# Other orders in a layer's opening and its linear attention, and value products issued one step later in the windowed attention

## The chip, the cores and the metric

The kernel runs on one core of one Trainium2 chip. The core has a matrix engine (TensorE, PE in the profile; its weight loads are PEld), a vector engine (VectorE, DVE), a scalar engine (ScalarE, ACT), a slower general engine (GpSimd, POOL) and a sequencer that issues transfers (SyncE, SP). They run side by side, each takes its own instructions in order, and they wait for each other with semaphores. Products are summed in PSUM, 8 banks of 128 x 512 numbers; everything else lies in SBUF. The metric is the device time of one execution in microseconds; the median of three runs counts.

## The reference, cut to what matters

One layer of a diffusion backbone: 256 latent tokens and 256 context tokens, width 2048, batch 1, one layer. Weights and activations are 32-bit.

```python
mod_x = split(silu(c) @ w_mod + b_mod, 6); mod_c = split(silu(c_ctx) @ w_mod + b_mod, 6)
h  = rms_norm(x, g_mix) * (1 + mod_x[1]) + mod_x[0]        # latent; the context likewise
qa, ka, va, qb, kb, vb, rb, lrf, lrb, gate_a, gate_b = split(h @ w_in)
gf = log_sigmoid(lrf @ w_gate_f + b_gate_f) / 16            # decay of the linear attention
gb = log_sigmoid(lrb @ w_gate_b + b_gate_b) / 16            # and of its backward direction
# A: windowed attention, 16 heads of 128 in 4 groups; a query block sees latent and context keys
o_attn = softmax([scores(qa, ka) in the window, scores(qa, cka), sink]) @ [va, cva]
# B: gated linear attention, 4 heads, keys 256 wide, values 512 wide, both directions
o_gla = latent_gla(qb, kb, vb, gf, gb, states left by the context)
y = sigmoid(gate_a) * (o_attn @ w_attn_o) + sigmoid(gate_b) * ((rms_norm(o_gla) * silu(rb)) @ w_gla_o)
x = x + mod_x[2] * (y @ w_out)
x = x + mod_x[5] * conv_ffn(rms_norm(x, g_ffn) * (1 + mod_x[4]) + mod_x[3])
```

## The kernel before

**Products.** Every large product is done in halves: an operand a is split into a rounded part and a remainder (`split`, line 60: a copy on ACT, a subtraction on DVE), and three products are summed, high by high, low by high, high by low. Weights come from memory as tiles of 256 x 512 numbers (`raw`, seven buffers, tag "raw"), and `wsplit_raw` (line 207) makes `whi` on ACT and `wlo` on DVE, three buffers each. `proj_T` (line 263) and `proj_nat` (line 222) go through a projection tile by tile. At the start of each weight tile they call `tick()`, and between its high and its low half `midway()` or a function given as `mid`. Eight tiles make a block of 512 columns, so a block has 16 such places, 0 to 15, even ones at a tile's start and odd ones in its middle. In blocks with 512-wide products a tile is 16 products ahead of its middle and 8 behind it.

**Side work.** `aside()` (line 156) advances a generator that stands in `beside`, by a rate: at each place the rate is added, and for each whole one the generator goes to its next `yield`. Matrix products of side work carry a lower bound, the last projection product issued (`pin`, `after`); apart from that a scheduler orders each engine's instructions when the program is built, by priority (program order) and by when it estimates their operands to be ready. In the opening (until `opening.clear()`, line 675) PE's order is the order of the program. `bank(..., side=True)` gives one of three PSUM banks for side work. SBUF tiles of side work come from tags with few buffers: "fa" four, "fb" four, "fc" six; large tiles from `big`, 16 buffers.

**The opening** (lines 531 to 675). Latent tokens `xr` are loaded, transposed; `square_sums` makes squares and adds them up with products by ones (`pr`), `factor_row` makes the norm's factors (`rrow`) of it. Shift and scale come column group by column group: `mod_both` (line 313) loads `mraw`, multiplies (`pm`), transposes on DVE (`mtr`), and its last step `end` folds with one more product (`pcol`) and copies into `scale1`, `shift1`. `groups` are 2, 2, 4, 4 and 4 of the 16 column tiles of the model's width. For group 0, `mods[0]` holds (a0, a1, ea) for the scale and (b0, b1, eb) for the shift. `idle(n)` issues n transposes of an identity that nobody reads (`warm`). `affine_scale` and `affine_shift` turn `xr` into h with its halves (`h00hi`, `h00lo`, ...), and the projections QB, KB and VB (queries, keys and values of the linear attention, first half) follow group by group; line 616's loop does groups 1 to 4. Within group 1 the eight steps of group 2's shift and scale are spread over six places (`steps`, `also`, `mid`, lines 631 to 649). All loads of the opening are issued by SP in the order of the program (`chain`).

**Linear attention** (lines 740 to 928). Four heads, one beside each of four projection blocks: head 0 beside the second half of the keys (`kb_block`), heads 1 to 3 beside the values (`v_block`). `gla_A` makes, as side work: four gates (two directions, two halves of the key width; product `pz`, four passes on ACT into `ge` and `gm`, an addition on DVE into `segs` and one on POOL into `gc`), then eight levels. Level lv builds decayed queries and keys (`q2`, `k2`) for segments of 2^lv tokens: exponentials on ACT, products and running sums (`segs`) on DVE; the products of the level before (`pa`) go to PE at the same time and are merged on DVE. Scans over the context (`kf`, `kg`) stand beside the levels. Behind the last level come the products with the context states, and `gla_o` multiplies with the values (`po`). With rate 0.97 the generator is first advanced at place 1: gates at places 1 to 4, levels 0 to 7 at 5 to 12, the last level's products at 13, nothing at 14, the context's products at 15.

**Windowed attention** (`attend`, line 1007). Beside a projection block, for two query blocks t: scores (`pS`) of four heads, softmax on DVE and ACT, and then for four key blocks k: four transposes (`ptp`), their split into `pth` and `ptl` (tag "fb"), three value products into `poa`. A `yield` stands behind k = 1 and k = 3.

The rest (projections of the outputs, merging, output projection, and the feed-forward part with its convolution) is not touched.

Of the kernel before, what the change touches and what calls it, by code (L numbers as in the profile page):

```python
# [31 lines left out]
def layer_kernel(ctx, tc, A, out):  # L32
# [280 lines left out]
    def mod_both(part, t0, n, dst, put=None):  # L313
# [5 lines left out]
        def step(k0):  # L319
            if k0 == 0:  # L320
                a.append(bank(f"pm{part}_{t0}", (P, w), side=True))
            raw = M("mraw", [P, nk, w])
            src = A["w_mod01"][part, t0 + k0 // nk].rearrange("p (c d) -> p c d", c=nk)
            if t0 < 4 and part == 0 and k0:
                load(raw[:, 0:nk // 2, :], src[:, 0:nk // 2, :])
                load(raw[:, nk // 2:nk, :], src[:, nk // 2:nk, :])
            else:
                load(raw, src)
            for k in range(nk):
                kt = k0 + k  # L330
# [97 lines left out]
    kbt = M("kb0", [P, 4, 512])  # L428
    vb0 = M("vb0", [P, 4, 512])

    def square_sums(s):

        pr = bank("pr", (P, T), side=True)
        parts, whole = [], None
        for i in range(4):
            x_ = xr[2 * s + i // 2][:, (i % 2) * 4:(i % 2) * 4 + 4, :]
            q = wr.tile([P, 4, T], F32, name="sq", tag="raw")
            if s + i:
                j = S.activation(q, x_, AF.Square).ins
                if s and i in (0, 2):  # L440
                    in_order(evicted[i + 1], j)
            else:
                V.tensor_tensor(q, x_, x_, op=ALU.mult)
                parts.extend(q[:, k, :] for k in range(4))
                continue
            h = q[:, 0:2, :]
# [91 lines left out]
    opening[:] = [pe_seq(PE.transpose(warm[:, 0:P], ident, ident)).ins]  # L538
# [12 lines left out]
    b0()  # L551
    affine_scale(0, *groups[0])
    idle(6)
    b1()
    raws = [first_w(i) for i in range(2)]
    idle(4)
# [59 lines left out]
    for gi, (t0, n) in enumerate(groups):  # L616
# [8 lines left out]
        if gi + 1 < len(groups):  # L625
# [2 lines left out]
            bg_rate[:] = [1.4 * len(bg_steps) / ticks + 0.01, 0.0]  # L628
            if gi == 1:
                bg_rate[:] = [0.0, 0.0]  # L630
                steps = iter([1, 2, 1, 4, 0, 0])

                def next_columns():
                    if pend:
                        pend.pop(0)()

                def scale_2():
                    next_columns()
                    for s in range(2):
                        affine_scale(s, *groups[2])  # L640

                also = iter([next_columns] * 3 + [scale_2, next_columns, lambda: affine_shift(0, *groups[2])])

                def mid():
                    pin[0] = last[0]
                    next(also)()
                    for _ in range(next(steps)):
                        bg_steps.pop(0)()
                    pin[0] = None
# [87 lines left out]
                         b.rearrange("p (f t) -> p f t", f=2), AF.Copy, scale=1.0 / 16)  # L737
        return eq

    def gla_A(h, kb, qb, res):  # L740
        k_ = kb[:, (h % 2) * 2:(h % 2) * 2 + 2, 0:T]
        kc = kb[:, (h % 2) * 2:(h % 2) * 2 + 2, T:2 * T]
        q_ = qb[:, 2 * h:2 * h + 2, :]
        R = M("segs", [P, 4, 2, T])
        PF, SB, SX, PX = (R[:, i] for i in range(4))
        G.memset(R[:, 2:4], 0.0)
        gc = []
        for d in range(2):
            g_ = W2("fc", "gc", [P, 2, T])
            for dt in range(2):  # L750
                f = 2 * h + dt
                pz = bank("pz", side=True)
# [5 lines left out]
                S.activation(mn, pz, AF.Relu, scale=-1.0, bias=b)  # L758
                S.activation(e, e, AF.Exp, scale=-1.0)
                S.activation(e, e, AF.Ln, bias=ones[:, 0:1])  # L760
                V.tensor_tensor((PF if d == 0 else SB)[:, dt, :], mn[:, 0:T], e[:, 0:T], op=ALU.add)
                G.tensor_tensor(g_[:, dt, :], mn[:, T:2 * T], e[:, T:2 * T], op=ALU.add)
                yield
            gc.append(g_)

        kf = W2("fb", "kf", [P, 2, T])
        kg = W2("fb", "kg", [P, 2, T])

# [87 lines left out]
            S.activation(dst, e, AF.Exp, scale=-1.0 / 16)  # L856
# [150 lines left out]
    def attend(g, qT):  # L1007
# [3 lines left out]
        for t in range(2):  # L1011
# [354 lines left out]
```

## Time and profile before

| | us |
|---|---|
| median of three runs | 1974.27 (1974.04 to 1974.33) |
| profiled execution, its own time | 1973.72 |
| its span, first to last instruction | 1972.0 |
| PE busy | 1952.8 |
| DVE busy | 1396.9 |
| ACT busy | 971.6 |
| stretch 0 to 207 us (opening) | PE busy 196.3 |
| stretch 207 to 462 us (linear attention) | PE busy 251.6 of 255 |
| stretch 584 to 787 us (most of the windowed attention) | PE busy 202.7 of 203 |

A row of the profile tells the place in the program (L95 is line 95; `mm_b`, which issues all products of side work, is L95, and `mm`, the projections, L83; transposes of side work are L98), the engine, the operation, what it writes and reads, and its form. In a timeline the first two numbers are the start from the span's beginning and the time until the last of the merged instructions ended, x is their count, and square brackets hold idle time of the engine before it and what ended that. In a list of waits the numbers are the total, the count and the longest. The end of a matmul is modelled, and matmuls overlap; their starts are measured. "fp32" products and transposes take other steps than the rounded "fp32r" ones of the projections.

### The profile page before, as it was taken

To read this page: it belongs to the slowest core of one execution; us is meant where nothing else is said; L and a number is where in the kernel's file an instruction comes from. 1 tells how busy PE (TensorE), PEld (TensorE's weight loads), DVE (VectorE), ACT (ScalarE), POOL (GpSimd) and SP (SyncE) were. 2 spreads that over 40 slices of the span, in tenths; PEclk is the share of its full clock that TensorE was granted. 3 is DMA by queue.
4 is the path that set the end of the run, shared out by engine and by line. 5 is a ranking of instruction groups with operands and counts; after the bars stand their busy time and mean duration, and the time that the engine had idled before them with its cause. 6 is when DMAs were issued, how large, how long until landed. Compare 5 with 4: busy or idle time off the path is not lost.

```text
span 1972.0 us, 27091 instructions
## 1 busy us (share of the span) xinstructions
PE 1952.8 (99%) x10304; PEld 1635.6 (83%) x10304; DVE 1396.9 (71%) x2150; ACT 971.6 (49%) x1415; POOL 39.9 (2%) x60
## 2 busy tenths in 40 slices
PE   8999999999999999999999999999999999999999
PEld 6679988888887777888888888888888888888887
DVE  5756855785768998777776467989886545677754
ACT  5223655462346565444444445755555334555533
POOL 0010000020000000000000000000000000000000
PEclk9999999999999999999999999999999999999999
DMA  9975222226654466899997677688786556666563
GB/s 392 412 255 176 69 66 71 79 84 210 212 162 126 129 208 220 297 299 307 312 310 237 238 246 252 193 276 284 263 275 224 192 193 191 186 188 191 188 212 114
DMA packets 182867, 420.90 MB, mean 213 GB/s; under 512 B 12512, under 2 KB 12736, under 8 KB 177744
## 3 DMA queue, kind: packets, MB, share of 16 engines
q1 hardware_dynamic: 181200, 413.45, 63.7%
q0 software_dynamic: 1360, 5.54, 1.0%
q8 instruction: 81, 1.33, 0.3%
q14 instruction: 50, 0.41, 0.1%
q10 hardware_dynamic: 176, 0.17, 0.0%
HBM read 416.98 MB, written 2.13 MB: 213 GB/s over the span
## 4 chain that ended last, share of the span: by engine, by line
PE 94%; DVE 3%; ACT 1%; DMA 1%; issue 1%; ACTq 0%; DVEq 0%
PE acc L83 72%; PE accs L83 12%; PE pa L95 2%; PE poa L95 1%; PE pS L95 1%; PE po L95 1%; PE pm L95 1%; DVE wlo L212 1%; PE ptp L98 1%; DMA mraw<-in_w_mod 1%; ACT whi L211 0%; DVE q L831 0%; PE pto L98 0%; DMA pack<-in_k_pack 0%; DVE k L838 0%
## 5 line engine op out<-in xcount | busy, mean ns | idle before, releaser
L212 DVE TENSOR_TENSOR wlo<-raw,whi 128x1024 fp32r<-128x1024 f32 x568 | 694.0, 1223 | 426.5 <-ACT whi L211 387.8
L211 ACT ACTIVATE whi<-raw 128x1024 fp32r<-128x1024 f32 x568 | 601.1, 1059 | 785.1 <-PE acc L83 605.0
L83 PE MATMUL accs<-h,whi 128*128 128x512 f32 x704 | 176.3, 392 | 0.0
L83 PE MATMUL acc<-h,whi 128*128 128x512 f32 x640 | 160.4, 392 | 0.0
L83 PEld LDWEIGHTS accs<-h,whi 128*128 128x128 f32 x704 | 126.6, 189 | 22.6
L83 PE MATMUL acc<-whi,h01hi 128*128 128x512 f32 x352 | 139.7, 397 | 0.0
L83 PE MATMUL acc<-whi,h00hi 128*128 128x512 f32 x352 | 139.2, 395 | 0.0
L83 PE MATMUL acc<-whi,h01lo 128*128 128x512 f32 x352 | 138.4, 393 | 0.0
L83 PE MATMUL acc<-whi,h00lo 128*128 128x512 f32 x352 | 137.6, 391 | 0.0
L83 PE MATMUL acc<-whi,al 128*128 128x512 f32 x352 | 137.0, 389 | 0.0
L83 PE MATMUL acc<-whi,ah 128*128 128x512 f32 x352 | 137.0, 389 | 0.0
L83 PEld LDWEIGHTS acc<-h,whi 128*128 128x128 f32 x640 | 115.1, 189 | 20.6
L83 PEld LDWEIGHTS accs<-h,wlo 128*128 128x128 f32 x704 | 96.0, 190 | 6.9
L83 PE MATMUL acc<-wlo,h01hi 128*128 128x512 f32 x352 | 99.0, 396 | 0.0
L83 PE MATMUL accs<-h,wlo 128*128 128x256 f32 x704 | 98.2, 282 | 0.0
L83 PE MATMUL acc<-wlo,h00hi 128*128 128x512 f32 x352 | 98.1, 394 | 0.0
L83 PE MATMUL acc<-wlo,ah 128*128 128x512 f32 x352 | 94.3, 389 | 0.0
L83 PEld LDWEIGHTS acc<-h,wlo 128*128 128x128 f32 x640 | 87.4, 190 | 6.3
L83 PE MATMUL acc<-h,wlo 128*128 128x256 f32 x640 | 89.4, 282 | 0.0
L376 DVE CUSTOM_DVE_ANT_0 raw<-raw,csrow,pack 128x1024 f32<-128x1024 f32 x64 | 81.2, 1278 | 0.0
L83 PEld LDWEIGHTS acc<-whi,al 128*128 128x128 f32 x352 | 66.1, 188 | 13.7
L83 PEld LDWEIGHTS acc<-whi,ah 128*128 128x128 f32 x352 | 66.1, 188 | 13.7
(376 smaller groups left out, 3553.0 us busy)
## 6 DMA issues: line engine op xcount, KB each, us to landing
raw<-in_w_in SPq DMA_DIRECT2D x204, 512.0 KB, 4.5
raw<-in_w_up SPq DMA_DIRECT2D x176, 512.0 KB, 4.2
raw<-in_w_modT SPq DMA_DIRECT2D x128, 512.0 KB, 4.6
raw<-in_w_down SPq DMA_DIRECT2D x88, 512.0 KB, 3.6
mraw<-in_w_mod SPq DMA_DIRECT2D x30, 1024.0 KB, 12.5
raw<-in_w_attn_o SPq DMA_DIRECT2D x32, 512.0 KB, 5.3
raw<-in_w_gla_o SPq DMA_DIRECT2D x32, 512.0 KB, 5.4
raw<-in_w_out SPq DMA_DIRECT2D x32, 512.0 KB, 4.4
```

The source lines that it names most:

```text
L83: r = pe_seq(PE.matmul(*a, **k))
L95: return pe_seq(after(PE.matmul(*a, **k)))
L98: return pe_seq(after(PE.transpose(*a)))
L211: j = S.activation(hi[:, 0:n, :], raw[:, 0:n, :], AF.Copy).ins
L212: i = V.tensor_tensor(lo[:, 0:n, :], raw[:, 0:n, :], hi[:, 0:n, :].bitcast(F32), op=ALU.subtract).ins
L376: i0 = V.tensor_tensor_reduce(out=raws[i], in0=raws[i], in1=row[0], scale=1.0, scalar=d if h else bmod[:, b0:b0 + 1], op0=ALU.mult, op1=AL ...
```

## The change

In the opening: the second half of the shift weights of groups 0 and 1 is loaded in one transfer instead of two; the product passes a0 and a1 stand between the sums of squares instead of behind them; 14 of the fillers are left out (6, 4 and 4 of 6); `gm1` is ordered behind the first square. In group 1, the fourth of the four steps at one place goes to the next place, and the folding of the shift with it to the one after.

In the linear attention: the gates become a generator of their own, `gla_gates`. Head 0 has its gates at places 0 to 3, its levels at 4, 6, 7, 8, 9, 10, 11, 12, and two gates of head 1 at 13 and 14. Heads 1 to 3 have their other two gates at 0 and 1, levels at 2, 4, 5, 7, 8, 10, 11, 12, the last level's products at 13, the context's products at 15, and the first two gates of the next head at 9 and 14. The rate is 1.

In the windowed attention: the three value products of key block k are issued behind the transposes and the split of block k + 1.

```diff
-            src = A["w_mod01"][part, t0 + k0 // nk].rearrange("p (c d) -> p c d", c=nk)
-            if t0 < 4 and part == 0 and k0:
-                load(raw[:, 0:nk // 2, :], src[:, 0:nk // 2, :])
-                load(raw[:, nk // 2:nk, :], src[:, nk // 2:nk, :])
-            else:
-                load(raw, src)
+            load(raw, A["w_mod01"][part, t0 + k0 // nk].rearrange("p (c d) -> p c d", c=nk))
...
-    add_up(0, 6)
-    V.tensor_scalar(gm1, gmix, -0.5, None, op0=ALU.mult)
+    add_up(0, 4)
+    in_order(squared[0], V.tensor_scalar(gm1, gmix, -0.5, None, op0=ALU.mult).ins)
     (a0, a1, ea), (b0, b1, eb) = mods[0]
+    a0()
+    add_up(4, 6)
+    a1()
     add_up(6, 9)
     factor_row(pr)
-    a0()
-    idle(6)
-    a1()
-    idle(4)
     ea()
     b0()
     affine_scale(0, *groups[0])
-    idle(6)
+    idle(2)
     b1()
...
-                steps = iter([1, 2, 1, 4, 0, 0])
+                steps = iter([1, 2, 1, 3, 1, 0])
...
-                also = iter([next_columns] * 3 + [scale_2, next_columns, lambda: affine_shift(0, *groups[2])])
+                def shift_2():
+                    next_columns()
+                    affine_shift(0, *groups[2])
+
+                also = iter([next_columns] * 3 + [scale_2, next_columns, shift_2])
...
-    def gla_A(h, kb, qb, res):
+    def gla_gates(h):
         R = M("segs", [P, 4, 2, T])
         G.memset(R[:, 2:4], 0.0)
         gc = []
+        yield R, gc
         for d in range(2):
-            g_ = W2("fc", "gc", [P, 2, T])
+            gc.append(W2("fc", "gc", [P, 2, T]))
             for dt in range(2):
...
-        yield
         yield
         pa = bank("pa", (P, 2, T), side=True)
...
+    def gate(h):
+        if h == 4:
+            return
+        if h not in gates:
+            it = gla_gates(h)
+            gates[h] = next(it), it
+        next(gates[h][1])
+
     def with_gla(h, kb, block):
-        res = []
-        beside[:] = [gla_A(h, kb, qbt, res), 0.97, 0.0]
+        res, own = [], []
+
+        def level():
+            if not own:
+                own.append(gla_A(h, kb, qbt, *gates[h][0], res))
+            next(own[0], None)
+
+        this, following = lambda: gate(h), lambda: gate(h + 1)
+        places = {i: [this] for i in ((0, 1, 2, 3) if h == 0 else (0, 1))}
+        for i in (4, 6, 7, 8, 9, 10, 11, 12) if h == 0 else (2, 4, 5, 7, 8, 10, 11, 12):
+            places[i] = [level]
+        places.update({13: [level], 14: [following], 15: [level]})
+        places.setdefault(13 if h == 0 else 9, []).append(following)
+
+        def along():
+            for i in range(16):
+                for fn in places.get(i, ()):
+                    fn()
+                yield
+
+        beside[:] = [along(), 1.0, 0.0]
...
+            def values(k, th, tl):
+                vk_h, vk_l = vah[:, k, g * P:(g + 1) * P], val[:, k, g * P:(g + 1) * P]
+                mm_b(po, vk_h, th, start=(k == 0), stop=False)
+                mm_b(po, vk_h, tl, start=False, stop=False)
+                mm_b(po, vk_l, th, start=False, stop=(k == 3))
+
+            ready = None
             for k in range(4):
...
                 split(th, tl, pf)
-                vk_h, vk_l = vah[:, k, g * P:(g + 1) * P], val[:, k, g * P:(g + 1) * P]
-                mm_b(po, vk_h, th, start=(k == 0), stop=False)
-                mm_b(po, vk_h, tl, start=False, stop=False)
-                mm_b(po, vk_l, th, start=False, stop=(k == 3))
+                if ready is not None:
+                    values(*ready)
+                ready = k, th, tl
                 if k in (1, 3):
                     yield
+            values(*ready)
```

More of the change, by code (lines that the diff above doesn't have):

```diff
@@ L429, in layer_kernel @@
     vb0 = M("vb0", [P, 4, 512])
+    squared = []
     def square_sums(s):
@@ L442, in square_sums @@
             else:
-                V.tensor_tensor(q, x_, x_, op=ALU.mult)
+                squared.append(V.tensor_tensor(q, x_, x_, op=ALU.mult).ins)
                 parts.extend(q[:, k, :] for k in range(4))
@@ L738, in q_evac @@
         return eq
-    def gla_A(h, kb, qb, res):
-        k_ = kb[:, (h % 2) * 2:(h % 2) * 2 + 2, 0:T]
-        kc = kb[:, (h % 2) * 2:(h % 2) * 2 + 2, T:2 * T]
-        q_ = qb[:, 2 * h:2 * h + 2, :]
+    def gla_gates(h):
         R = M("segs", [P, 4, 2, T])
-        PF, SB, SX, PX = (R[:, i] for i in range(4))
         G.memset(R[:, 2:4], 0.0)
         gc = []
+        yield R, gc
         for d in range(2):
-            g_ = W2("fc", "gc", [P, 2, T])
+            gc.append(W2("fc", "gc", [P, 2, T]))
             for dt in range(2):
@@ L760, in gla_A @@
                 S.activation(e, e, AF.Ln, bias=ones[:, 0:1])
-                V.tensor_tensor((PF if d == 0 else SB)[:, dt, :], mn[:, 0:T], e[:, 0:T], op=ALU.add)
-                G.tensor_tensor(g_[:, dt, :], mn[:, T:2 * T], e[:, T:2 * T], op=ALU.add)
+                V.tensor_tensor(R[:, d, dt, :], mn[:, 0:T], e[:, 0:T], op=ALU.add)
+                G.tensor_tensor(gc[d][:, dt, :], mn[:, T:2 * T], e[:, T:2 * T], op=ALU.add)
                 yield
-            gc.append(g_)
+    def gla_A(h, kb, qb, R, gc, res):
+        k_ = kb[:, (h % 2) * 2:(h % 2) * 2 + 2, 0:T]
+        kc = kb[:, (h % 2) * 2:(h % 2) * 2 + 2, T:2 * T]
+        q_ = qb[:, 2 * h:2 * h + 2, :]
+        PF, SB, SX, PX = (R[:, i] for i in range(4))
         kf = W2("fb", "kf", [P, 2, T])
@@ L903, in layer_kernel @@
         q_evac(i // 2)(i % 2, qb0[i])
-    def with_gla(h, kb, block):
-        res = []
-        beside[:] = [gla_A(h, kb, qbt, res), 0.97, 0.0]
+    gates = {}
+    def gate(h):
[5 more added lines that the diff above has]
+        next(gates[h][1])
+    def with_gla(h, kb, block):
+        res, own = [], []
[15 more added lines that the diff above has]
+        beside[:] = [along(), 1.0, 0.0]
         v = block()
```

## The prediction

> **What bounds the kernel.** I read the page first (busy time and the chain that ended last), then who waited for whom, then the timeline of TensorE (PE) at the places that the change touches.
>
> ```profile
> PE 1952.8 (99%) x10304; PEld 1635.6 (83%) x10304; DVE 1396.9 (71%) x2150; ACT 971.6 (49%) x1415; POOL 39.9 (2%) x60
> PE 94%; DVE 3%; ACT 1%; DMA 1%; issue 1%; ACTq 0%; DVEq 0%
> ```
>
> PE is the bound: 1952.8 of 1972.0 us busy, 94% of the chain. The change removes no product, so all that it can win is time in which PE stood still, and the fillers of the opening. The page's own list of PE's waits is short:
>
> ```profile
> PE warm L538 <- DMA pack<-in_k_pack: 6.7, 1, 6.7
> PE pa L95 <- DVE k L838: 2.6, 6, 0.5
> PE pm L95 <- DMA mraw<-in_w_mod: 1.2, 1, 1.2
> PE pa L95 <- DVE q L831: 0.7, 1, 0.7
> ```
>
> The first is the start and stays. The second and fourth are the linear attention (`pa`, the products of one level), the third is one load in the opening. The listed waits are too small, because the end of a matmul is modelled:
>
> ```profile
> 299.52 0.39 PE L83 MATMUL acc<-whi,h01lo 128*128 128x512 f32 x1
> 300.42 1.13 PE L95 MATMUL pa<-q,k 128*128 128x128 f32 x8 [0.51 <-DVE k L838]
> ...
> 304.35 0.39 PE L83 MATMUL acc<-whi,h11lo 128*128 128x512 f32 x1
> 304.58 1.05 PE L95 MATMUL pa<-q,k 128*128 128x128 f32 x8
> 305.38 0.48 PE L83 MATMUL acc<-wlo,h01hi 128*128 128x512 f32 x1
> ```
>
> Products of 512 columns follow each other every 0.23 us (304.35, 304.58), though each is drawn 0.39 us long. So a listed wait hides 0.16 us more, and the visit that had to wait is 0.08 us longer (1.13 against 1.05). Seven waits in linear attention: 2.6 + 0.7 + 7 x 0.24 = **5.0 us**. All are in heads 1 to 3, none in head 0.
>
> **Part 1, linear attention: gates of the next head early, levels spread.** Why are those products late? Busy time by stretch in head 1's block (columns: length, then PE, PEld, DVE, ACT, POOL, clock, DMA):
>
> ```profile
> 270.00:282.00 12.00, 12.00 (x54) 9.95 (x53) 4.80 (x7) 11.41 (x19) 2.81 (x3) 1.00 0.23 64
> 282.00:300.40 18.40, 17.91 (x99) 15.10 (x98) 17.89 (x41) 10.31 (x25) 0.97 (x1) 1.00 0.23 72
> 300.40:313.70 13.30, 12.96 (x73) 11.01 (x73) 13.11 (x27) 6.75 (x15) 0.95 (x1) 1.00 0.28 81
> 313.70:324.00 10.30, 10.30 (x48) 8.70 (x48) 3.69 (x7) 3.68 (x8) 0.00 (x0) 1.00 0.18 52
> ```
>
> While the eight levels run, VectorE (DVE) is busy 31.0 of 31.7 us; in the 12 us before, 4.8, and in the 10.3 us after, 3.7. ScalarE (ACT) is full before the levels, with the gates (11.4 of 12). The levels are a ladder of DVE work squeezed into two thirds of the block. The change starts it earlier: two of a head's four gates are made in the block before, level 0 moves from place 5 of the 16 to place 2, and the levels stand at 2, 4, 5, 7, 8, 10, 11, 12 where they stood at 5 to 12. Places are the starts and middles of the eight weight tiles, so their times can be read from today's gates and visits:
>
> ```profile
> 272.28 0.39 PE L95 MATMUL pz<-wgl 128*128 128x512 f32 x1
> ...
> 278.18 0.39 PE L95 MATMUL pz<-wgl 128*128 128x512 f32 x1
> 282.03 1.05 PE L95 MATMUL pa<-qb,kb 128*128 128x128 f32 x8
> ```
>
> ```profile
> 276.25 0.43 DVE L761 TENSOR_TENSOR segs<-gm,ge 128x256 f32<-128x256 f32 x1 [1.43 <-ACT ge L760]
> ...
> 282.31 0.42 DVE L761 TENSOR_TENSOR segs<-gm,ge 128x256 f32<-128x256 f32 x1 [0.18 <-ACT ge L760]
> 283.92 0.69 DVE L831 TENSOR_TENSOR q<-q,qb 128x512 f32<-128x512 f32 x1
> ```
>
> Place 2 is 272.28, place 4 is 278.18, place 5 is 282.03. With two gates instead of four, the last gate's DVE add, which opens the ladder, comes where the second one comes now: 276.25 instead of 282.31, 6.1 us earlier; up to 2 us more, since the gates start at place 0 and not 1. The tightest demand is the first: level 0's products now go at place 4 (278.18 plus one visit at place 2 of 0.8, so 279.0), and their operand is ready at 283.92 + 0.69 = 284.6 today: 5.6 us earlier is needed, 6.1 to 8.1 are there. Later levels need less: today's late products at 300.42 are those of level 4, due at place 10 in both orders, with a ladder that runs 6 us ahead. So the waits go, less something at places 8 and 12, which follow the level before by a half tile only: I take **4.6 us** of the 5.0; bounds 0 and 5.0.
>
> What the move issues: the gates' products (one of 512 columns each) are the same number. A gate puts four ACT passes, a DVE add and a POOL add into places 9, 13 and 14 of the block before; there DVE has its idle 6.6 us and ACT as much (the stretch 313.7 to 324). The next head's `segs` must have a buffer then, and today it comes free late:
>
> ```profile
> POOL segs L746 <- ACT q L856: 31.3, 1, 31.3
> ```
>
> POOL waits for the exponentials behind the last level (L856) before it may clear head 3's `segs`. So for heads 2 and 3 the add of the gate at place 9 will wait until about place 13. That costs nothing while it ends inside its own block; queued behind it are the gate at 14 (same small buffers) and nothing of PE's. Without that cover, the head falls back to the late ladder (rival below).
>
> POOL's adds now fall beside the ladder. What POOL does to DVE stands in head 3, where it prepares the rotary tables:
>
> ```profile
> 301.33 0.42 DVE L841 TENSOR_TENSOR segs<-segs 128x256 f32<-128x256 f32 x1
> ...
> 426.25 1.44 POOL L943 TENSOR_TENSOR att<-rope,norms 128x128 f32<-128x128 f32 x1
> 427.30 0.68 DVE L841 TENSOR_TENSOR segs<-segs 128x256 f32<-128x256 f32 x1
> ```
>
> The same add takes 0.68 us instead of 0.42. A few such collisions per head are some 0.5 to 1 us of DVE time, inside the 0.5 to 2.5 us of lead. The Trainium skill (SBUF — State Buffer, "Who interferes with whom") goes further: a VectorE instruction with two SBUF inputs and a GpSimd one that reads SBUF exclude each other for a whole instruction. By that rule each of the three moved POOL adds could hold the ladder for its full length, and the sum would be some 4 instead of 4.6; the trace's rows, where the DVE add grew by 0.26 and not by POOL's whole 1.44, are milder, and I go by them.
>
> **Part 2, the opening.** It is paced by transfers (windows, PE alone; last columns clock, DMA share, GB/s):
>
> ```profile
> 18.00:24.00 6.00, 5.41 (x57) 1.00 1.04 423
> 70.00:110.00 40.00, 39.77 (x292) 1.00 1.01 402
> 110.00:120.00 10.00, 10.00 (x57) 1.00 0.01 4
> ```
>
> Until 110 us the DMA engines are full, so no load can land earlier than it does; PE can only stop waiting for one. The chain of the first microseconds:
>
> ```profile
> 15.71 0.81 PE warm L535 x6
> 16.52 1.00 PE pm L95 x16
> 17.52 0.59 PE warm L535 x4
> ...
> 19.21 0.81 PE warm L535 x6
> 20.01 1.00 PE pm L95 x16
> ```
>
> ```profile
> 19.52 0.33 SPq L104 DMA_DIRECT2D mraw<-in_w_mod  x1
> ```
>
> 14 of the 38 fillers go: 0.81 + 0.59 + two thirds of 0.81 = 1.9 us of PE. But the second half of the shift weights, used at 20.01, landed about when SP's next issue, which waits for its semaphore, went out (19.52). PE can come 0.5 us earlier, not 1.9; the rest becomes idle time ahead of that load. The sums of squares (`pr`) move behind the first two weight passes; they end about 1 us later, still before that landing. Joining the two half loads into one changes no bytes: nothing. I carry 0.3 us, since the next loads bind again; bounds 0 and 0.5 (the clock is a rival).
>
> ```profile
> 62.56 2.74 PE L95 MATMUL pm<-mraw,cS 128*32 128x512 f32 x21
> 66.52 1.07 PE L95 MATMUL pm<-mraw,cS 128*32 128x512 f32 x8 [1.22 <-DMA mraw<-in_w_mod]
> 67.51 0.38 PE L83 MATMUL acc<-h00hi,wlo 128*128 128x256 f32 x1
> ```
>
> ```profile
> 67.58 2.10 PE acc L83 x16
> ```
>
> The last row is of the chain of waits. Here is the listed wait: the fourth weight step of that place stands until its load lands at 66.5. The new counts (3, 1 for 4, 0) put these 16 products, 2.1 us, ahead of it; PE then reaches the load at about 67, after its landing. Won: 1.22 + 0.16 = 1.4. Paid: a group of eight of its own (66.52 to 67.51, 0.99, against 2.74 - 0.16 by three, 0.86, in a run) and one change of number format more, 0.1 each way: 0.35. The shift columns and their affine pass then come in the middle of the last block of that group, some 2.8 us before the products that read them; the path through DVE and ACT takes about 2. Sum of the opening: 1.4 - 0.35 + 0.3 = **1.3 us**. After 120 us loads follow PE's pace again, so the gain is kept.
>
> **Part 3, cross attention.** Today the three value products of step k are issued behind their own split; the weight loads (PEld) for them wait:
>
> ```profile
> PEld poa L95 <- ACT pth L61: 4.2, 17, 0.3
> PEld poa L95 <- DVE ptl L62: 2.4, 10, 0.3
> ```
>
> 27 short waits, 6.6 us, but PE's own list shows none: projection products were put between. The change issues them one step later, when the split is done. I take a tenth, **0.7 us**. Upper bound 2.0 (27 waits with 0.07 each on PE). Lower bound -1.0: a product behind a fp32 transpose is 0.09 us late (305.38: 0.48 against 0.39), and a dozen more such changes would cost that. All four small buffers are then held across a step; the next split waits for them as it does now.
>
> **Sum.** 4.6 + 1.3 + 0.7 = 6.6 us. The profiled execution took 1973.72 us for a span of 1972.0; so 1965.4 of span, 1967.1 of time, and against the median of the runs, which lies 0.55 higher at 1974.27: **1967.7 us**.
>
> **Rivals.**
> - *The lateness only moves.* DVE's 31 us of ladder stay; if ACT, not the gates' place, opens it, the waits reappear at places 4, 8 and 12. For: DVE is at 98% in that stretch. Against: 12 us of the block with DVE at 40%. 1974.27 - 1.3 - 0.7 = 1972.3.
> - *Loads hide the opening.* DMA is at 1.01 to 110 us; if PE then only waits at another landing, 1.3 is lost: 1969.0. Against: between 70 and 110 PE is 39.77 of 40 busy.
> - *The clock falls in the opening.* The fillers kept PE going while loads were awaited; without them it stands up to 1.7 us at a time. The granted clock was 1.00 throughout, so no row prices it; PE work of 3 us at half speed would turn +1.3 into about -2: 1971.0. The Trainium skill (TensorE: Matmul & The Clock Gate, "A second HAM failure mode") tells of clocks that swing when PE idles briefly between groups; no run here shows it yet.
> - *Slower: the first rung.* Level 0's products stand at place 4. If the ladder opens only 1.5 us earlier (gates behind the head before's evictions on ACT, or `segs` late), PE waits there 5.6 - 1.5 = 4.1 us in each of three heads, 12.3, against 5.0 + 2.0 saved: 1979.6. It is slower from an advance below 3.3 us. For: ACT is 95% busy there now. Against: most of that is the four gates, of which two leave.
>
> **Chances.** Forecast 0.60 (1965.0 to 1970.2 by the bounds of its terms), lateness moves 0.15, loads 0.10, clock 0.07, first rung 0.08. A measurement of this kernel tells about 0.2%, 4 us, from no change: faster is below 1970.3. Forecast and loads, less their upper tails: 0.69; slower 0.07; the same 0.24. Range 1964.3 to 1973.3: it takes in the lateness and leaves out the first rung and the tails.
>
> **What would show it.** Right: no `pa` wait for DVE in heads 1 to 3, DVE nearer to even over a block; no PE wait for `mraw` at 66 us, the first projection product some 0.4 us earlier; fewer PEld waits of `poa`. Wrong: a `pa` wait at place 4, a gate's pass blocking ACT at a block's end, a clock under 1 before 30 us, or an opening that ends at the same time for want of loads.

## The result, and the profile after

| | before | after |
|---|---|---|
| median of five runs, us | 1974.27 (1974.04 to 1974.35) | 1966.45 (1966.13 to 1966.61) |
| profiled execution, its own time | 1973.72 | 1966.47 |
| its span | 1972.0 | 1964.7 |

The ratio is 0.9961, with a 95% interval of 0.9949 to 0.9972, so the gain is small (0.4%) but clear of no change: 7.8 us by the medians and 7.3 by the two spans. The forecast was 1967.7.

The page of the kernel after (busy time and instructions), and its list of what PE waited for (total, count, longest):

```profile
PE 1949.7 (99%) x10290; PEld 1636.2 (83%) x10290; DVE 1398.3 (71%) x2150; ACT 971.9 (49%) x1413; POOL 37.9 (2%) x60
```

```profile
PE warm L535 <- DMA pack<-in_k_pack: 6.4, 1, 6.4
PE pm L95 <- DMA mraw<-in_w_mod: 0.7, 2, 0.5
...
PE acc L83 <- ACT h00hi L508: 0.7, 2, 0.5
```

No wait of `pa` is left. The 1.2 us for `mraw` at 66 us are gone, and 0.7 us stand at two other loads (at 18.61 and 37.67 us); the wait for `h00hi` now has two places. To see which part won what, take three tiles of PE that each kernel has once at a known place: `plb` stands at the end of the opening, `ptk` behind the linear attention, `pt_gate` behind the windowed attention. Before, then after (durations in ns, then the first and last start in us):

```profile
L713 PE MATMUL plb<-shift,wlr x32: 167/171/189, 200.4 to 200.7; 128*32 128x2 f32 x32
L98 PE MATMUL ptk<-pack,sq x16: 270/272/275, 511.0 to 529.1; 128*128 128x128 f32 x16
L98 PE MATMUL pt_gate<-pack,gcol x2: 271/272/273, 1155.5 to 1506.6; 128*16 128x128 f32 x2
```

```profile
L713 PE MATMUL plb<-shift,wlr x32: 167/171/189, 199.6 to 199.8; 128*32 128x2 f32 x32
L98 PE MATMUL ptk<-pack,sq x16: 270/272/275, 504.6 to 522.7; 128*128 128x128 f32 x16
L98 PE MATMUL pt_gate<-pack,gcol x2: 271/272/273, 1148.1 to 1499.2; 128*16 128x128 f32 x2
```

The lead over the kernel before is 0.8 to 0.9 us behind the opening, 6.4 behind the linear attention, 7.4 behind the windowed attention, and stays so to the end. By parts: **opening 0.9** (forecast 1.3), **linear attention 5.5** (4.6), **windowed attention 1.0** (0.7). Below, "the lead" is always this difference, taken at the same, n-th projection product of two traces.

**Linear attention.** Windows of head 1's block after (length, PE, PEld, DVE, ACT, POOL, clock, DMA), then DVE and PE at the first rung of the ladder:

```profile
278.20:298.30 20.10, 20.10 (x106) 17.24 (x105) 17.72 (x39) 9.70 (x23) 0.00 (x0) 1.00 0.28 79
298.30:313.00 14.70, 14.70 (x82) 12.74 (x81) 12.00 (x24) 8.49 (x18) 0.74 (x1) 1.00 0.25 72
```

```profile
274.57 0.43 DVE L758 TENSOR_TENSOR segs<-gm,ge 128x256 f32<-128x256 f32 x1
275.04 0.85 DVE L842 TENSOR_TENSOR segs<-segs 128x256 f32<-128x256 f32 x1
275.81 0.68 DVE L832 TENSOR_TENSOR q<-q,qb 128x512 f32<-128x512 f32 x1
```

```profile
278.16 1.05 PE L95 MATMUL pa<-q,kb 128*128 128x128 f32 x8
```

From the first rung's products on, DVE is busy 29.7 of 34.8 us; counted from the ladder's first work on DVE (274.5 to 309.7 us) it is 32.7 of 35.2, against 31.0 of 31.7 before. So the ladder has more room, but not much. The last gate's addition comes at 274.57 where it came at 282.31, level 0's operand is ready at 276.5, and its products go at 278.16 without a wait: 1.7 us of slack.

**Opening.** PE at the first loads and at the end of group 1 (timeline):

```profile
18.61 1.07 PE L95 MATMUL pm<-mraw,cS 128*32 128x256 f32 x16 [0.53 <-DMA mraw<-in_w_mod]
...
20.74 0.23 PE L95 MATMUL pcol<-mtr,pack 128*32 128x16 f32 x2 [0.47 <-DVE mtr L330]
...
22.46 0.38 PE L83 MATMUL acc<-h00hi,whi 128*128 128x256 f32 x1 [0.46 <-ACT h00hi L508]
...
73.77 1.06 PE L95 MATMUL pm<-mraw,cS 128*32 128x512 f32 x8
75.03 0.39 PE L83 MATMUL acc<-h00hi,whi 128*128 128x256 f32 x1 [0.19 <-ACT h00hi L508]
75.54 0.39 PE L83 MATMUL acc<-h00lo,whi 128*128 128x256 f32 x1
```

The same two places before:

```profile
23.30 0.39 PE L83 MATMUL acc<-h00hi,whi 128*128 128x256 f32 x1 [0.46 <-ACT h00hi L511]
...
75.45 1.06 PE L95 MATMUL pm<-mraw,cS 128*32 128x512 f32 x8
76.45 0.39 PE L83 MATMUL acc<-h00hi,whi 128*128 128x256 f32 x1
76.67 0.28 PE L83 MATMUL acc<-h00lo,whi 128*128 128x256 f32 x1
```

The first projection product comes 0.84 us earlier (22.46 against 23.30). With the wait at 66 us gone, the lead is 1.68 at the weight products (73.77 against 75.45). Then PE stands: 0.26 us longer ahead of `h00hi`, and 0.51 instead of 0.22 ahead of `h00lo`, and a little ahead of each of the next few. By 80 us the lead is 0.86. One trace is not the whole story here: four kernels have this same opening (after, and `open_only`, `gates_own` and `levels_old` below), and their first product comes at 22.04 to 22.46 us, their lead behind the opening is 0.9 to 1.2 us; this trace has the smallest. DVE after says why the lead shrinks at 75 us:

```profile
20.25 0.44 DVE L330 STREAM_TRANSPOSE mtr<-pm 128x256 f32<-128x256 f32 x1
...
71.83 0.67 DVE L340 COPY shift<-pcol 32x8 f32<-32x8 f32 x4 [2.45 <-PE pcol L95]
72.53 0.69 DVE L518 TENSOR_TENSOR vb<-vb,acc 128x512 f32<-128x512 f32 x1
73.14 1.22 DVE L212 TENSOR_TENSOR wlo<-raw,whi 128x1024 fp32r<-128x1024 f32 x1
74.27 0.16 DVE L343 TENSOR_TENSOR shift<-shift,pack 128x8 f32<-128x8 f32 x1
74.35 0.68 DVE L518 TENSOR_TENSOR vb<-vb,acc 128x512 f32<-128x512 f32 x1
75.01 1.69 DVE L509 SCALAR_TENSOR_TENSOR h00lo<-xr,shift,h00hi 128x256 fp32r<-128x256 f32 x4
```

Between the copies of the shift columns and the small addition that ends them stand an eviction and a weight split of other work, 1.8 us, and another eviction ahead of `h00lo`.

**Windowed attention.** The weight loads of the value products waited 17 and 10 times before; after:

```profile
PEld poa L95 <- ACT pth L61: 2.6, 10, 0.3
...
PEld poa L95 <- DVE ptl L62: 1.9, 8, 0.4
```

That these waits are what was won is not shown. I took PE's starts in the stretch from 584 to 790 us and counted what lies beyond 0.2275 us for a product of 512 columns and 0.058 for a transpose. Before, the 28 entries from a projection product into `poa` that do not follow a transpose closely lost 0.15 us in all; the nine that come one product behind a transpose lost 0.15 each, where a projection product at that place loses 0.09. So waits for weight loads cost PE 0.7 us there at most. The larger difference is that PE goes over from rounded products to transposes 69 times before and 55 times after (before, 21 transposes stand alone; after, one), and the time beyond the steps around these changes falls from 13.6 to 11.8 us. The other steps grow by 0.9.

### The profile page after: what moved, and what is told of

Same layout as the page of the kernel before. It is cut to its first block, busy times and chain, and to the rows that moved or that the text cites. A ratio compares the mean times of both kernels' runs of the same rounds, so it can differ in the third digit from the quotient of the medians.

```text
span 1964.7 us, 27066 instructions
## 1 busy us (share of the span) xinstructions
PE 1949.7 (99%) x10290; PEld 1636.2 (83%) x10290; DVE 1398.3 (71%) x2150; ACT 971.9 (49%) x1413; POOL 37.9 (2%) x60
## 4 chain that ended last, share of the span: by engine, by line
PE 97%; DVE 1%; ACT 0%; DMA 0%; issue 0%; DVEq 0%
PE acc L83 75%; PE accs L83 13%; PE pa L95 2%; PE poa L95 1%; PE pm L95 1%; PE pS L95 1%; PE po L95 1%; PE ptp L98 1%; DVE wlo L212 0%; PE pto L98 0%; PE pr L459 0%; DMA pack<-in_k_pack 0%; ACT whi L211 0%; PE ptq L98 0%; PE pz L95 0%
## 5 line engine op out<-in xcount | busy, mean ns | idle before, releaser
L83 PEld LDWEIGHTS acc<-whi,h00hi 128*128 128x128 f32 x352 | 66.2, 188 | 13.7 <-issue 0.8
```

The costliest lines, as they stand in the source:

```text
L83: r = pe_seq(PE.matmul(*a, **k))
```

## The experiments

All medians in us, 5 rounds unless said. The kernel before, run beside them, had 1974.18, 1974.07 and 1974.28 in the three sets.

### Each part alone

The kernel before with the hunks of one part of the diff, and nothing else:

```diff
# gla_only
+    def gla_gates(h):
...
+        places.update({13: [level], 14: [following], 15: [level]})
# open_only
+    a0()
+    add_up(4, 6)
+    a1()
...
+                steps = iter([1, 2, 1, 3, 1, 0])
# att_only
+            def values(k, th, tl):
...
+            values(*ready)
```

> The kernel before with the linear attention's new order alone (gates as a generator of their own, two of a head's four in the block before, levels at the new places); the opening and the windowed attention stay as they were. Theory, read from the two traces: the lead of the kernel after grows by 5.5 us between 204 and 465 us, so this part alone gives 1974.3 - 5.5 = 1968.8 us, with no wait of pa for DVE left. The prediction's own term, 4.6, gives 1969.7. Rival: part of the lead hangs on the moved opening, which shifts the weight tiles against the levels; then this part alone gives under 4 us, above 1970.3.

> The kernel before with the opening's edits alone (sums of squares, fillers, joined load, steps 3 and 1 for 4 and 0). Theory, read from the traces: 0.9 us, 1973.4. The prediction's term is 1.3, 1973.0. Rival: the opening is paced by its loads and gives nothing, 1974.3; in that case the lead of 0.8 us at the first projection product is gone by 110 us.

> The kernel before with the value products of the windowed attention one step later, alone. Theory, read from the traces: 1.0 us, 1973.3. The prediction's term is 0.7, 1973.6. Rival: the gain of 1.0 us seen in that stretch comes from the phase into which the linear attention's new order brings it; alone it gives nothing, 1974.3 or more by a dozen changes of number format at 0.09 us each (1975.3).

Measured: 1968.65 (5.5 us faster than before; ratio 0.9971, 0.9959 to 0.9982), 1972.83 (1.35; 0.9994, 0.9985 to 1.0003) and 1972.94 (1.24; the same interval). For the last two the interval holds no change, so their traces carry more than their times. Linear attention alone, opening alone, windowed attention alone:

```profile
L713 PE MATMUL plb<-shift,wlr x32: 167/171/189, 200.6 to 200.9; 128*32 128x2 f32 x32
L98 PE MATMUL ptk<-pack,sq x16: 270/272/275, 505.6 to 523.7; 128*128 128x128 f32 x16
```

```profile
L713 PE MATMUL plb<-shift,wlr x32: 168/171/189, 199.4 to 199.6; 128*32 128x2 f32 x32
```

```profile
L98 PE MATMUL ptk<-pack,sq x16: 270/272/273, 510.9 to 529.0; 128*128 128x128 f32 x16
L98 PE MATMUL pt_gate<-pack,gcol x2: 271/272/273, 1154.4 to 1505.5; 128*16 128x128 f32 x2
```

The lead goes from -0.2 to 5.4 across the linear attention, to 1.0 in the opening, and from 0.1 to 1.1 across the windowed attention. These are the sizes in the whole; the three gains in time add up to 8.1 us where the whole has 7.8. Within that 0.3 us, no part's gain hangs on another.

### Linear attention: early gates or spread levels?

```diff
# gates_own
-        places = {i: [this] for i in ((0, 1, 2, 3) if h == 0 else (0, 1))}
+        places = {i: [this] for i in ((0, 1, 2, 3) if h == 0 else ())}
...
-        places.update({13: [level], 14: [following], 15: [level]})
-        places.setdefault(13 if h == 0 else 9, []).append(following)
+        if h:
+            places.update({0: [this, this], 1: [this, this]})
+        places.update({13: [level], 15: [level]})
# levels_old
-        for i in (4, 6, 7, 8, 9, 10, 11, 12) if h == 0 else (2, 4, 5, 7, 8, 10, 11, 12):
+        for i in (4, 6, 7, 8, 9, 10, 11, 12) if h == 0 else (5, 6, 7, 8, 9, 10, 11, 12):
```

> The kernel after, but heads 1 to 3 make all four gates in their own block again, two at place 0 and two at place 1; levels and all else as after. Theory (the early gates open the ladder): four gates are 11.4 us of ACT, so the last addition of a gate comes some 2 us earlier than before instead of 6 to 8, and by the prediction's rival of the first rung PE waits at place 4 for level 0, 5.6 - 2 = 3.6 us in each of three heads: 1966.5 + 10.8 = 1977. Rival: it is the levels' places that count, and the order of PE puts a late level's products behind more projection products; then under 2 us is lost: below 1968.5.

> The kernel after, but the levels of heads 1 to 3 stand at the places 5 to 12 again; the early gates stay. Theory (the ladder opens with the last gate's addition, and DVE takes a level when its operands are there): the ladder still opens about 6 us earlier, no wait of pa comes back, and the time is that of after, 1966.5 within 0.5. Rival (the places hold the levels): DVE takes level 0 only when place 5 has come, the ladder runs at the old time, and the 5.0 us of waits come back: 1971.4.

Measured: gates_own 1970.27 (3 rounds; 1970.15 to 1970.66), levels_old 1968.53 (1968.45 to 1968.61). Neither theory nor rival: 3.8 and 2.1 us are lost, so each half of the new order is worth something and neither does it alone. With the gates in their own block, the waits of PE, the last gate's addition on DVE, and the first rung of head 2 on PE:

```profile
PE pa L95 <- DVE q L832: 2.1, 3, 0.8
```

```profile
279.91 0.97 DVE L758 TENSOR_TENSOR segs<-gm,ge 128x256 f32<-128x256 f32 x1
```

```profile
343.72 1.13 PE L95 MATMUL pa<-q,kb 128*128 128x128 f32 x8 [0.80 <-DVE q L832]
```

The gate comes 5.3 us later than in after, and a wait stands at level 0 of each head, as the first-rung rival said. But it is 0.5 to 0.8 us and not 3.6: PE's order, made when the program is built, puts those products some 4 us later (282.42 in head 1, against 278.16), behind projection products. Such a rung is priced by what is left after that.

With the levels at their old places (PE's waits; then DVE):

```profile
PE pa L95 <- DVE k L839: 0.9, 3, 0.3
```

```profile
275.55 0.68 DVE L832 TENSOR_TENSOR q<-q,qb 128x512 f32<-128x512 f32 x1
...
281.70 0.42 DVE L801 TENSOR_SCALAR at<-pa 128x256 f32<-128x256 f32 x1 [0.91 <-PE pa L95]
```

DVE does take level 0 long before its place (275.55, as in after), so the ladder opens early. Then it runs out: DVE stands for 0.91 us until PE has made its first level's products, which now come at place 5, and later the levels of one a place are late again at 305.82 (0.35 us). That the four small buffers of `q2` and `k2` hold it there was not tried.

Summed over all visits of `pa` and `pz` in the four blocks, PE's time beyond 0.23 us for each product of 512 columns, 0.12 for 256 and 0.06 for 128 is 22.5 us before, 17.3 after, 21.0 and 19.6 in these two: 3.7 and 2.2 more than in after, as the times say. (The `pa` products themselves follow each other by 0.11 us, so most of each sum is no wait; only the differences count.)

### Opening, the end of group 1

```diff
# shift_first: the shift's addition ahead of the eviction and the split; also
# (in the first microseconds) mtr ahead of the second scaling of the tokens
+                    hold.append(column_add[0])
+                    urgent[:] = [column_add[0]]
...
+    in_order(folded[0], scaled)
# dve_order: the whole order written out, and the same second line
+            in_order(column_add[0], sums[0], los[0], los[1], sums[1])
+            hold[:] = [sums[1]]
...
+                in_order(i, los[2], los[3], sums[2], sums[3])
# steps_back
-                steps = iter([1, 2, 1, 3, 1, 0])
+                steps = iter([1, 2, 1, 4, 0, 0])
```

`column_add` is the shift's addition, `sums` the four evictions of VB, `los` the four `h00lo`, `i` the next weight split; `hold` orders that split behind what it holds.

> The kernel after with two orders on DVE changed: in group 1 the addition that ends the shift columns of group 2 goes ahead of the eviction addition and the split that stand between it and its copies (72.5 to 74.3 us in the trace), and in the first microseconds the transposition of the shift sums goes ahead of the second scaling of the tokens (20.25 us). Theory: the opening's missing gain is queueing on DVE, 0.8 us at the second place (waits for h00hi and h00lo at 75.0 us) and about 0.35 at the first, so 1966.45 - 1.15 = 1965.3 us, and the waits of acc for h00hi fall away. Rival: the loads bind again before 110 us, and PE waits there instead: 1966.4 us, with the same lead after 120 us.

> The kernel after with the whole DVE order written out around the end of group 1: addition of the shift columns, first eviction of VB, two h00lo, second eviction, the split of the next weights, two h00lo, the last two evictions; and the transposition of the shift sums ahead of the second scaling in the first microseconds. The run with only the shift's addition put first traded the wait for h00hi for one on the second eviction (0.53 us at 76.33). Theory (DVE's order there is what eats the opening's gain, and a place exists for each): no wait of PE is left between 74 and 80 us, the lead over the kernel before stays near 2.0 us from 77 us to 204, and the time is 1966.4 - 0.9 = 1965.5. Rival (DVE is simply full from 71.5 to 80 us, and any order pays): a wait of the same 0.5 to 0.9 us comes up at another product before 85 us, and the time stays at 1966.4.

> The kernel after with the steps of group 1 at their old places (four at the one place, none at the next, and the shift columns at the start of the last block). Theory (the moved step wins about 1 us at the load and DVE's order behind it takes all but 0.1 of it back): PE waits 1.2 to 1.4 us for mraw near 66 us and not for h00hi at 75; 1966.6 within 0.3. Rival (the prediction's term): the moved step is worth 1.05 us, 1967.5.

Measured: shift_first 1966.44, dve_order **1965.52** (1965.41 to 1965.61), steps_back 1966.85 (1966.82 to 1966.98). The first was a miss: `h00lo` came at 74.02 instead of 75.01, but the second eviction then came too late, and PE waited for its bank:

```profile
76.33 0.39 PE L83 MATMUL acc<-h00hi,whi 128*128 128x256 f32 x1 [0.53 <-DVE vb L523]
```

With the whole order written out, no wait is left there, and the lead at `plb` is 1.8 us, against 0.9 to 1.2 in the four traces with the opening of after:

```profile
74.64 0.39 PE L83 MATMUL acc<-h00hi,whi 128*128 128x256 f32 x1
74.86 0.28 PE L83 MATMUL acc<-h00lo,whi 128*128 128x256 f32 x1
```

```profile
L732 PE MATMUL plb<-shift,wlr x32: 167/171/189, 198.6 to 198.9; 128*32 128x2 f32 x32
```

So DVE was not full there, it was out of order. This version beats both kernels: against before 0.9957 (0.9944 to 0.9969), and its slowest run (1965.61) is ahead of the fastest of after (1966.13), though the two stood in different sets, and the kernel before was 0.2 us faster in this one. With the old steps the wait for the load is back:

```profile
65.77 1.07 PE L95 MATMUL pm<-mraw,cS 128*32 128x512 f32 x8 [1.42 <-DMA mraw<-in_w_mod]
```

The moved step is worth 0.4 us by the times as it was written. Between 60 and 80 us the lead falls by 0.3 in steps_back, grows by 0.1 in after, and by 0.9 in dve_order: with DVE in order the same edit is worth 1.2 by this difference. No run has that order together with the old steps.

### Opening, the first microseconds

```diff
# fillers_back: six, four and four fillers; fillers_b1: the last line alone
     a0()
+    idle(6)
     add_up(4, 6)
     a1()
+    idle(4)
...
-    idle(2)
+    idle(6)
     b1()
# pr_first
-    add_up(0, 4)
+    add_up(0, 6)
...
-    a0()
-    add_up(4, 6)
-    a1()
     add_up(6, 9)
     factor_row(pr)
+    a0()
+    a1()
# halves_back
+                load(raw[:, 0:nk // 2, :], src[:, 0:nk // 2, :])
+                load(raw[:, nk // 2:nk, :], src[:, nk // 2:nk, :])
```

> The kernel after with the 14 fillers put back: six behind a0, four behind a1, four more ahead of b1. The sums of squares stay between the weight passes. Theory (the path to the first projection product runs through PE there): the last sums of squares end 1.4 us later, the norm's factors and the scaled tokens with them, and the first product comes 1.0 to 1.4 us later: 1967.5 to 1967.9. The prediction's term for the fillers, 0.3, gives 1966.8. Rival (the load of b1 and the clock decide): the first product comes less than 0.4 us later, and the granted clock of the first 30 us is the same with and without the fillers; 1966.5 to 1966.8.

> The kernel after with four fillers put back ahead of b1 only (six there, as before); the ten between a0, a1 and the sums of squares stay out. In the trace of after PE stands 0.53 us there for the load of b1 (18.61 us), and four fillers are 0.54 us. Theory (the loss with all 14 back came through the sums of squares behind the other ten, and from the granted clock, 0.62 from 42 to 45 us in that profile): no change, 1966.45 within 0.3. Rival (fillers as such cost, or the clock falls with them): above 1967.0, with a granted clock under 0.9 in some stretch before 60 us.

> The kernel after with the sums of squares back ahead of both weight passes a0 and a1, and no fillers there. Theory (the load of b1 at 18.6 us and the loads around 37 us bind): the norm's factors come 2 us earlier, the transposition of the shift sums is no longer queued behind the scaling of the tokens, the first product comes about 0.35 us earlier than in after, and by 50 us that is gone again at the next load: 1966.2 to 1966.5. Rival (moving the sums is what won the opening): the first product comes later than in after by 0.5 or more, 1967.0 or above.

> The kernel after with the second half of the shift weights of groups 0 and 1 loaded in two transfers again. The prediction's term for joining them is nothing: 1966.45. Rival: one transfer lands sooner than two, since SP issues one instruction less and PE waits for one landing less; then b1 starts later than 18.61 us by 0.3 or more and the time is 1966.8 or above.

Measured: fillers_back 1969.22 (1968.46 to 1969.43), fillers_b1 1966.97 (1966.72 to 1967.19), pr_first 1966.43, halves_back 1966.76 (1966.63 to 1966.86).

All 14 fillers cost 2.8 us, twice what was expected. The first product is 1.4 us behind that of after (23.85), 0.46 of which stands already in PE's first wait (6.82 against 6.36 us); the other half is the clock (windows of fillers_back, PE, then granted clock, DMA share, GB/s):

```profile
40.00:44.00 4.00, 3.11 (x18) 0.84 1.05 389
44.00:48.00 4.00, 4.00 (x30) 0.73 1.03 422
```

From 30 to 50 us this trace loses 1.5 us more. The four fillers ahead of `b1` are not free either: `b1` starts at 18.96 instead of 18.61, and 0.5 us is lost, against an expected 0.3 at most; the clock stays at 1.00. But PE is late there before it comes to them: its first wait ends at 6.62 instead of 6.36, and the product pass ahead of these fillers ends 0.50 us later than in after (18.15 against 17.65). PE's first wait goes with the number of fillers in all 14 traces: 6.2 to 6.4 us in the nine kernels with 24, 6.6 in the one with 28, 6.7 to 6.8 in the four with 38. Why is open. The place of the sums of squares moves nothing. Two half loads instead of one cost 0.3 us (the ranges of the runs do not overlap, though the lowest of these, 1966.63, and the highest of after, 1966.61, nearly meet). PE waits twice:

```profile
17.70 0.64 PE L95 MATMUL pm<-mraw,cS 128*32 128x256 f32 x8 [0.16 <-DMA mraw<-in_w_mod]
19.01 0.64 PE L95 MATMUL pm<-mraw,cS 128*32 128x256 f32 x8 [0.67 <-DMA mraw<-in_w_mod]
```

These waits are not where it is lost: the second eight products begin at 19.01 us, and the ninth of the sixteen in after at 19.07, because PE does the first half while it waits; the rival's sign, a later `b1`, did not come. It is lost by 40 us, where the lead falls from 1.4 to 0.7 us: PE stands for 0.43 us ahead of 34.57, where it does not in after, and 0.26 instead of 0.20 for the load at 37.83. From 12 to 24 us the DMA engines moved less with two halves (windows of halves_back, then of after: PE, clock, DMA share, GB/s):

```profile
12.00:24.00 12.00, 10.35 (x96) 1.00 1.01 403
12.00:24.00 12.00, 10.40 (x101) 1.00 1.01 414
```

So it is in all 14 traces: 401 to 404 GB/s in the four kernels with the halves, 414 to 417 in the ten with the joined loads. The difference, 12 us of some 12 GB/s, is about 0.14 MB, or 0.35 us at 410 GB/s, an estimate that fits the 0.3.

Over the traces with the new opening, fillers_back aside, the lead at the first product varies from 0.3 to 1.4 us, and at 50 us from 0.3 to 1.2: 1.4 becomes 0.9 in dve_order and 0.7 in halves_back. The next loads, which PE awaits at 37 us (0.20 us at 37.67 in after), take back most of what exceeds about one.

## Why the prediction was right or wrong

**The bound and the seven waits: right.** The listed waits are too small by 0.24 us each, so 5.0 and not 3.3 us stood in them; all seven are gone, and the part gave 5.5, alone and in the whole. The step that was too careful is "less something at places 8 and 12": nothing stayed there, so the 0.4 held back were won too, and 0.3 more came from head 0, where one wait, listed with 0.07 us, had stood that the prediction counted as none. The last 0.2 is not assigned.

**The first rung: right, and why.** "6.1 to 8.1 are there" was 7.7 (282.31 to 274.57), of which 5.6 were needed; 0.9 of the 7.7 is the lead of the opening, which moves the products too, so 6.9 count. gates_own, with less lead, shows the rival's wait at the place where the rival put it, at a third of its price: by the rows above, PE's order had moved.

**"The add of the gate at place 9 will wait until about place 13": wrong, without cost.** Its product went at 296.29 and its addition at 300.85, before place 11 (the products at 302.87); `segs` was not late, and the list of POOL's waits no longer has the wait of 31.3 us.

**POOL beside the ladder: the row was misread.** It was read as a milder collision, 0.26 us. POOL's row for the addition at 275.04 above:

```profile
274.62 0.98 POOL L759 TENSOR_TENSOR gc<-gm,ge 128x256 f32<-128x256 f32 x1 [0.72 <-ACT ge L757]
```

POOL ends at 275.60 and DVE's addition at 275.89, 0.29 behind it, though it began at 275.04. In the pair of rows that the prediction showed, POOL ends at 427.69 and DVE at 427.98: 0.29 again. So DVE stood until POOL was done; its row is the shorter the later it began. That is what the Trainium skill says (SBUF — State Buffer, "Who interferes with whom"): a DVE instruction with two SBUF inputs and a POOL one that reads SBUF exclude each other for a whole instruction. The prediction made a sum of 4 of that rule, and the part gave 5.5. Such stands were there before too: DVE's additions at 276.79 and 282.77 took 0.78 and 0.84 us instead of 0.42. In head 1's block they add up to 0.8 us before and 1.6 after, and the ladder had 1.7 us of slack at its first rung. That the slack is what hid them is argued; no run varied it.

**The opening: 0.9 for 1.3, by two errors of opposite sign.** First, "landed about when SP's next issue went out (19.52)" was wrong: PE waits for that load in after and has it at 18.61, and with two halves, as before, at 19.01 (halves_back). So the first product came 0.84 us earlier (0.84 to 1.26 in the four traces) and not some 0.4. Two premises were wrong as well. That "no load can land earlier than it does" does not hold: with the joined loads the engines moved 414 to 417 GB/s instead of 401 to 404, and joining, a term put at nothing because it "changes no bytes", is worth the 0.3 us of halves_back. The constants, too, landed earlier with fewer fillers (PE's first wait, 6.36 against 6.68); how much of the 0.84 that makes was not separated. The sums of squares end 1.9 us later and not 1 (16.6 instead of 14.7); that is still before the landing, but the scaling behind them held `mtr` (20.25) and PE for 0.47 us. With that undone (dve_order) the next loads take it back.

Second, the step "some 2.8 us before the products that read them; the path through DVE and ACT takes about 2" failed. The path took 3.5 us from `pcol` (71.55) to the first `h00lo` (75.01), because the estimate took the instructions and not the queue: DVE had an eviction, a split and another eviction between them. The term for the moved step, 1.4 - 0.35 = 1.05, was right in size: dve_order shows 1.2. As written it came to 0.4.

**Windowed attention: size near, mechanism not shown.** 27 waits of weight loads became 18, and the part gave 1.0 instead of 0.7, inside its bounds of -1.0 to 2.0. But 0.7 was a tenth of the waits, a guess and not a reading, and PE's steps show the largest gain at changes between transposes and rounded products, of which there are 14 fewer, and at most 0.7 us of waits for weight loads that could be won. The lower bound had taken a dozen more such changes. So that this term came out so near is in part luck.

**The sum.** 5.5 + 0.9 + 1.0 = 7.4 for 6.6. The other 0.5 us between 1967.7 and 1966.45 is the step by which the profiled execution of before was 0.55 faster than the median; in after the two agree. The forecast's "1965.0 to 1970.2 by the bounds of its terms" does not come out of these bounds: 5.0 + 1.55 + 2.0 and 0 + 1.05 - 1.0 give 1965.7 to 1974.2.

**The rivals.** The lateness did not move, and no first rung came. Loads hide only what goes beyond about 1 us of the opening. The clock stayed at 1.00 without the fillers. By the Trainium skill (TensorE: Matmul & The Clock Gate, "A second HAM failure mode") it may swing where PE idles briefly between groups. The one swing seen here came with more fillers in, not fewer.

## What to carry to other kernels

Price a wait of PE by the step to the next start, not by the listed gap, and price a moved step by the queue of the engine that must serve it: here the order of ten DVE instructions was worth 0.9 us. A ladder of dependent levels needs both, an early opening and places with room between them; taking either away cost 2.1 to 3.8 of the 5.5 us. Count what fillers cost before putting them ahead of a load: here four cost 0.5 us and fourteen 2.8, and more than half of that shows elsewhere, in the first wait and in the clock.

## What the runs showed of the hardware that was not expected

In fillers_back the granted clock fell to 0.84 and 0.73 between 40 and 48 us, right behind two stands of PE (0.42 and 0.67 us at 40 to 41 us). The kernel before has nearly the same two (0.37 and 0.67 at 39.5 to 40.4) and this in its windows:

```profile
40.00:44.00 4.00, 3.43 (x32) 1.00 1.05 386
44.00:48.00 4.00, 4.00 (x25) 1.00 1.05 429
```

So short stands alone do not decide it, and what does is open: only one execution of each was profiled.

Two more came out of the opening. With two loads of 512 KB joined into one of 1 MB, the DMA engines moved 414 to 417 GB/s between 12 and 24 us (ten traces); with the halves it was 401 to 404 (four traces). And the constants, the first load that PE waits for, landed later in the programs with more fillers (6.2 to 6.4, 6.6, 6.7 to 6.8 us with 24, 28 and 38 of them); the cause is open.
